# Second norm of a one-layer backbone taken in two token halves, with wider modulation rows

## The chip, the cores and the metric

The kernel runs on one core of a Trainium2 chip. Its engines work side by side: TensorE (PE, with its weight loads PEld), VectorE (DVE), ScalarE (ACT), GpSimd (POOL) and SyncE (SP); here POOL and SP mostly issue transfers. The metric is the device time of one launch in microseconds (us), the median of several.

## The reference

One layer (256 latent tokens, 256 context tokens, width 2048), float32, weights in float32:

```python
sh1_x, sc1_x, g1_x, sh2_x, sc2_x, g2_x = split(silu(c) @ w_mod + b_mod, 6)   # adaLN; the same from c_ctx
hx = rmsnorm(x) * norm1_g * (1 + sc1_x) + sh1_x          # hc from the context tokens
zx, zc = hx @ w_in + b_in, hc @ w_in + b_in
mix = concat(s5(zx, zc), conv(zx), mlstm(zx, zc))        # three groups of heads
x = x + g1_x * (mix @ w_out)
hx2 = rmsnorm(x) * norm2_g * (1 + sc2_x) + sh2_x         # the second norm
x = x + g2_x * (silu(hx2 @ w_g) * (hx2 @ w_u)) @ w_ffn_out   # width 5632
out = rmsnorm(x) * norm_f_g
```

## The kernel before, in words

Activations lie with features on the partitions and the 256 tokens along the free side, in 16 row tiles (`KT`). All big weights come as one stream of 128x128 tiles in the order in which they are used (`tile_order`), eight to a chunk of 512 KB. SP fetches chunk c into one of three `raw` buffers; ACT rounds it to float32r (`whi`, a 128x1024 cast, L511) and DVE subtracts to get the rest (`wlo`, L477), three buffers each. A product is three float32r matmuls: `whi*hhi`, `whi*hlo`, `wlo*hhi` (`mm3`, L609), each with its own weight load; `mm2` (L616) takes hi and lo of the activations in one matmul of 512 columns. So TensorE walks through the stream once: first the S5, conv, key, value (V), query (Q) and gate columns of `w_in`, then the GLU, `w_out` in two passes, and the feed-forward in eight blocks.

A product of the other kind, in plain float32 (`native=True`: norm sums, S5, attention), is recorded as two matmuls.

Beside the stream run jobs, written as generators and stepped by a pump (`Sched`): the S5 scan, the conv, the attention and the modulation (`mod_job`, L1037), which makes the gate, shift and scale vectors of `w_mod` that the layer's second half needs (quarters q = 0 to 3). For q = 0 it uses TensorE. For q = 1 to 3 it takes blocks of 512 columns: 16 steps on DVE that add weight row times scalar into an accumulator (`macc`, L488; the first step on ACT), then four transposes on TensorE (L1067) and four sums on ACT. POOL fetches its weights (`wm`, 512 KB each, three buffers).

`Arrange` (L152) then makes the final order of every engine's queue from a list schedule with costs written by hand; the order is fixed, and each engine works through its own in turn. A matmul on float32r costs `6 + 0.4427 * cols` ns there (L288), an ACT copy `190 + 0.84 * n`. `ranks` shifts an instruction's priority, `pins` ties it to the one before it.

After the first stage, `s5_moves` (L1091) turns `zT` into `U` by sixteen 32x512 copies, half on DVE (L492), half on ACT (L511). In V (L1341) each pass of four banks ends with four additions on DVE into `vx`, which free the banks; the first Q product takes the next bank of the tag `m`.

Around the second norm: the second pass over `w_out` makes 16 tiles `ct` of `xres`, 24 matmuls of 256 columns each; `SumSq` (L1508) squares each on ACT and sums over features on TensorE. After ct = 15 come `rsqrt` (L625: Ln and Exp on ACT, three DVE operations), `make_h2` for row tile 0 (L1557) and the feed-forward's first block, which runs over `kt` with eight weight tiles (24 matmuls) for each `kt`, into four banks.

Of the kernel before, what the change touches and what calls it, by code (L numbers as in the profile page):

```python
# [17 lines left out]
D = 2048  # L18
# [28 lines left out]
MOD_PE = {(0, b) for b in range(4)}  # L47
# [57 lines left out]
C_ID, C_MF, C_MR, C_K, C_SELG, NCST = 0, 128, 256, 384, 512, 640  # L105
# [46 lines left out]
class Arrange:  # L152
# [122 lines left out]
    def account(self, k, i, e, size):  # L275
# [8 lines left out]
        elif e == "PE":  # L284
# [4 lines left out]
            if any(x[1].startswith(("whi", "wlo")) for x in size):  # L289
                self.main.add(k)  # L290
# [162 lines left out]
def hybrid_layer_kernel(ctx: ExitStack, tc: tile.TileContext, xt, ctxt, wm1, wmr, wst, wg, bvrow, pvd, cstd, s5p, out):  # L453
# [21 lines left out]
    def tt(o, a, b, op):  # L475
        sc.dve += 62 + 1.05 * n_of(o)
        return V.tensor_tensor(out=o, in0=a, in1=b, op=op)  # L477

    def ts(o, a, s1, op0, s2=None, op1=None):
        if op1 is None:  # L480
            V.tensor_scalar(o, a, s1, None, op0=op0)
        else:
            V.tensor_scalar(o, a, s1, s2, op0=op0, op1=op1)
        sc.dve += 62 + 0.6 * n_of(o)

    def stt(o, a, s, b, op0, op1):
        sc.dve += 62 + 1.05 * n_of(o)
        return V.scalar_tensor_tensor(o, a, s, b, op0=op0, op1=op1)  # L488
# [13 lines left out]
    def act(o, a, f, bias=0.0, scale=1.0, pin=False):  # L502
        i = S.activation(o, a, f, bias=bias, scale=scale)  # L503
# [5 lines left out]
    def acopy(o, a):  # L509
        sc.act += 190 + 0.84 * n_of(o)  # L510
        return S.copy(o, a)  # L511

# [3 lines left out]
    def mm(o, l, r, start, stop, native=False, tp=None, sgc=False, pin=False):  # L516
# [7 lines left out]
        sc.pe += (max(n * 4, 512) if native else max(n, 256)) / 2.36 / (1 if tp is None else 4)  # L524
# [21 lines left out]
    cst = sb.tile([128, C_SELG], F32, name="cst")  # L546
# [7 lines left out]
    maskf = cst[:, C_MF:C_MF + 128]  # L554
    maskr = cst[:, C_MR:C_MR + 128]
# [18 lines left out]

    def split(c):
        his[c] = sb.tile([128, CH * 128], F32R, name="whi", tag="whi", bufs=3)
        ahead(U_SPLIT, acopy(his[c], raw[c]))
        los[c] = sb.tile([128, CH * 128], F32R, name="wlo", tag="wlo", bufs=3)
        ahead(U_SPLIT, tt(los[c], raw[c], his[c], OP.subtract))
        for d in (raw, his, los):  # L580
            d.pop(c - 4, None)
# [43 lines left out]
    def rsqrt(o, ps, n, scale, eps, epsv):  # L625
# [3 lines left out]
        act(y, y, AF.Exp, scale=-0.5)  # L629
        stt(t, y, -0.5 * scale, y, OP.mult, OP.mult)  # L630
# [126 lines left out]
    def s5_params():  # L757
# [7 lines left out]
        def expo(x, e, em1):  # L765
            n, r, p = t(), t(), t()
# [6 lines left out]
            ni = pre.tile([128, 32], I32, name="ni", tag="ni")  # L773
            V.tensor_copy(ni, n)
            V.tensor_copy(n, ni.bitcast(F32))
# [7 lines left out]
            used[0] -= 3  # L783
# [132 lines left out]
    for kt in range(KT):  # L916
# [8 lines left out]
        if kt == 13:  # L925
            phase1[0] = False
            keep(nc.sync.dma_start(cst[:, 128:], cstd[:, 128:C_SELG]))
# [108 lines left out]

    def mod_job():  # L1037
      for q in range(4):
        while mst["go"] < q:
            yield 500  # L1040
        for b in range(4):
            on_pe = (q, b) in MOD_PE
            acc = sb.tile([128, 512], F32, name="macc", tag="macc", bufs=1)
            if on_pe:
                psm = bbank()
            for kp in range(0, 8, 2):
                w = [wm.pop((q, b, kp + i)).rearrange("p (k n) -> p k n", k=2) for i in range(2)]
                for j in range(4):
                    kt = 2 * kp + j
                    wj = w[j // 2][:, j % 2, :]  # L1050
                    s = cs[:, kt, 0:1]
                    if on_pe:
                        mm(psm[32 * j:32 * j + 32, :], cs[:, kt, :], wj, kt < 4, kt >= 12, native=True, tp=(0, 32 * j),
                           pin=j > 0)
                    elif kt == 0:
                        act(acc, wj, AF.Copy, scale=s, pin=q == 3)
                    else:
                        stt(acc, wj, s, acc, OP.mult, OP.add)
                mod_dma()
                mod_dma()  # L1060
                yield 2 * (MOD_PACE if on_pe else MOD_PACE_D if q < 3 else MOD_PACE_F)
            dst = mods[:, q, 4 * b:4 * b + 4]
            if on_pe:
                acopy(acc, psm)
# [4 lines left out]
            if on_pe:  # L1069
                rsum(dst, ps.rearrange("p (f j r) -> p f j r", f=4, j=4)[:, :, :, 0])  # L1070
            else:
                for j in range(4):
                    S.activation(acc[:, 128 * j:128 * j + 128], ps[:, 128 * j:128 * j + 128], AF.Copy,
                                    accum_out=dst[:, j:j + 1])
                    sc.act += 390
# [265 lines left out]
    for cb in range(2):  # L1341
        pss = [mbank(), mbank(), mbank(), qbank()]
# [12 lines left out]
        for t in range(4):  # L1355
# [8 lines left out]
    hn = RH[:, 6144:8192].rearrange("p (j n) -> p j n", j=2)  # L1364

# [141 lines left out]
    stt(A2, mods[:, 2, :], 1.0, pvc("n2g", 0, 16), OP.add, OP.mult)  # L1507
    class SumSq:  # L1508


        def __init__(self):
            self.b = bank("qk", 2)
            self.sq = []
            self.n = 0
# [9 lines left out]
        def sums(self):  # L1524
            if self.n <= 12 and len(self.sq) == 4:
# [4 lines left out]
                if self.n == 12:  # L1530
                    e = tmp(256)
                    acopy(e, self.b[:, 0:256])
                    mm(self.b[:, 256:512], r32.to_broadcast([128, 128]), e, True, False, native=True)
            elif self.n > 12:
                mm(self.b[:, 256:512], ones, self.sq.pop(0), False, self.n == KT, native=True)
            return self.b[:, 256:512]

    s2 = SumSq()
    for ct in range(KT):
# [4 lines left out]
        if ct == 14:  # L1544
            lnexp()
# [3 lines left out]
    stp = s2.sums()  # L1549

# [3 lines left out]
    rsqrt(rs2, stp, 256, 1.0 / D, eps6, 1e-6)  # L1554
    h2 = sb.tile([128, KT, 2, NT], F32R, name="h2", tag="hc")

    def make_h2(kt):  # L1557
        xn, h = tmp(256), tmp(256)
        tt(xn, xres[:, kt, :], rs2, OP.mult)
        act(h2[:, kt, 0, :], xn, AF.Identity, bias=mods[:, 1, kt:kt + 1], scale=A2[:, kt:kt + 1])  # L1560
        ts(h, xn, A2[:, kt:kt + 1], OP.mult, mods[:, 1, kt:kt + 1], OP.add)
        tt(h2[:, kt, 1, :], h, h2[:, kt, 0, :], OP.subtract)
# [19 lines left out]
    def ffn_in(b):  # L1582
# [3 lines left out]
        if b == 0:  # L1586
            pss = [mbank(), mbank(), mbank(), qbank()]
            for kt in range(KT):
# [161 lines left out]
```

## Time and profile before

| | us |
|---|---|
| three runs, median | 1446.77 (1446.09 to 1446.86) |
| the profiled execution, its own time | 1447.56 |
| its span, first to last instruction | 1445.8 |
| TensorE busy | 1404.1 (97%) |
| DVE busy | 1049.0 (73%) |
| ACT busy | 738.3 (51%) |
| mean granted TensorE clock | 0.993 |

A row of the timeline gives start, duration, engine, line, operation and tiles; in brackets, how long the engine was idle before it and what it waited for. A duration of a matmul includes its way through the pipeline, so the time that one costs in a stream is read from start to start, or from a stretch of time divided by the matmuls in it.

### The profile page before, as it was taken

What the parts mean: (1) busy time and instruction counts of PE and PEld (TensorE: products, weight loads), DVE (VectorE), ACT (ScalarE), POOL (GpSimd) and SP (SyncE); (2) the same over time, 40 slices, a digit from 0 to 9 for tenths busy, and PEclk for the clock granted to TensorE, in tenths of its full rate; (3) what the DMA queues carried; (4) which work ended last, traced back from release to release, by engine and by line L of the source; (5) the groups of instructions that cost most, each with busy time, mean ns of one, the idle gap of its engine ahead of it and who ended that gap; (6) DMA issues with size and microseconds to landing.
All of it is one profiled execution on the core that took longest, in us unless ns stands there. A gap on an engine that the chain in (4) does not pass through costs nothing.

```text
span 1445.8 us, 25513 instructions
## 1 busy us (share of the span) xinstructions
PE 1404.1 (97%) x9920; PEld 1234.9 (85%) x9920; DVE 1049.0 (73%) x1944; ACT 738.3 (51%) x1302; POOL 107.7 (7%) x207
## 2 busy tenths in 40 slices
PE   5999999999999999998999999999999999999996
PEld 3888888987879999997998888888888888888885
DVE  8555699998878877988787778566555665556665
ACT  5334887666664445445555545534444334444353
POOL 1221111110001101111010000000000000000000
PEclk9999999999999999999999999999999999999998
DMA  9997564453427667788478787555555555555553
GB/s 370 382 350 292 184 218 145 166 181 127 149 77 293 214 234 269 246 302 290 161 276 275 255 286 261 187 186 184 189 188 189 189 190 188 187 184 186 190 176 115
DMA packets 87929, 315.50 MB, mean 218 GB/s; under 512 B 10096, under 2 KB 10736, under 8 KB 87808
## 3 DMA queue, kind: packets, MB, share of 16 engines
q1 hardware_dynamic: 60912, 216.80, 44.3%
q0 software_dynamic: 26896, 97.07, 18.8%
q8 instruction: 78, 1.28, 0.3%
q14 instruction: 43, 0.35, 0.1%
HBM read 311.73 MB, written 2.10 MB: 217 GB/s over the span
## 4 chain that ended last, share of the span: by engine, by line
PE 74%; issue 14%; DMA 4%; DVE 3%; POOL 2%; ACT 2%; SPq 0%; POOLq 0%; DVEq 0%; ACTq 0%
PE ps_m L520 48%; PE ps_qk L520 18%; PE ps_b L520 8%; DMA wm<-in_wmr_dram 2%; POOL wm L650 1%; DVE macc L488 1%; DMA wmu<-in_wm_dram 1%; DVE wlo L477 1%; DMA wmt<-in_wm_dram 1%; DMA cr<-in_ctxt_dram 1%; ACT whi L511 1%; DMA raw<-in_wst_dram 0%; ACT U L511 0%; POOL wmu L650 0%; PE ps_b L1160 0%
## 5 line engine op out<-in xcount | busy, mean ns | idle before, releaser
L477 DVE TENSOR_TENSOR wlo<-raw,whi 128x1024 fp32r<-128x1024 f32 x386 | 471.5, 1222 | 263.7 <-ACT whi L511 257.7
L511 ACT CAST whi<-raw 128x1024 fp32r<-128x1024 f32 x386 | 403.8, 1047 | 460.3 <-PE ps_m L520 231.7
L520 PE MATMUL ps_m<-h,whi 128*128 128x512 f32 (+1 forms) x800 | 252.1, 369 | 3.6 <-ACT h L503 3.5
L520 PE MATMUL ps_m<-ffa,whi 128*128 128x512 f32 x704 | 248.2, 395 | 0.0
L520 PE MATMUL ps_qk<-h,whi 128*128 128x512 f32 (+1 forms) x688 | 232.8, 383 | 0.0
L520 PE MATMUL ps_m<-h,wlo 128*128 128x256 f32 x704 | 199.6, 284 | 0.0
L520 PE MATMUL ps_m<-ffa,wlo 128*128 128x256 f32 x704 | 198.4, 282 | 0.0
L520 PE MATMUL ps_m<-hx,whi 128*128 128x256 f32 x960 | 186.3, 290 | 5.1 <-ACT hx L503 3.1
L520 PE MATMUL ps_qk<-h,wlo 128*128 128x256 f32 x656 | 185.5, 283 | 0.0
L520 PEld LDWEIGHTS ps_m<-h,whi 128*128 128x128 f32 x800 | 145.0, 190 | 30.4 <-ACT h L503 3.9
L520 PEld LDWEIGHTS ps_m<-hx,whi 128*128 128x128 f32 x960 | 148.2, 189 | 20.3 <-issue 15.3
L520 PEld LDWEIGHTS ps_m<-ffa,whi 128*128 128x128 f32 x704 | 132.3, 188 | 31.8 <-issue 1.2
L520 PEld LDWEIGHTS ps_qk<-h,whi 128*128 128x128 f32 x688 | 127.0, 188 | 27.1
L488 DVE SCALAR_TENSOR_TENSOR macc<-wm,cs,macc 128x512 f32<-128x512 f32 x180 | 134.3, 746 | 11.8 <-DMA wm<-in_wmr_dram 8.3
L520 PE MATMUL ps_m<-hx,wlo 128*128 128x256 f32 x480 | 136.5, 284 | 0.6 <-DVE wlo L477 0.6
L520 PEld LDWEIGHTS ps_m<-h,wlo 128*128 128x128 f32 x704 | 133.1, 189 | 0.0
L520 PEld LDWEIGHTS ps_m<-ffa,wlo 128*128 128x128 f32 x704 | 132.2, 188 | 0.1
L520 PEld LDWEIGHTS ps_qk<-h,wlo 128*128 128x128 f32 x656 | 123.3, 188 | 0.0
L650 POOL DMA_DIRECT2D wm<-in_wmr_dram x128 | 67.5, 528 | 585.1 <-DVE macc L488 436.4
L488 DVE SCALAR_TENSOR_TENSOR xres<-ps_m,mods,xres 128x256 f32<-128x256 f32 x160 | 76.9, 481 | 33.2 <-PE ps_m L520 31.2
L520 PEld LDWEIGHTS ps_m<-hx,wlo 128*128 128x128 f32 x480 | 90.6, 189 | 3.0 <-issue 2.1
L488 DVE SCALAR_TENSOR_TENSOR XB<-XB,pv 128x256 f32<-128x256 f32 x120 | 54.0, 477 | 0.4
(271 smaller groups left out, 2109.2 us busy)
## 6 DMA issues: line engine op xcount, KB each, us to landing
raw<-in_wst_dram SPq DMA_DIRECT2D x386, 512.0 KB, 3.6
wm<-in_wmr_dram POOLq DMA_DIRECT2D x128, 512.0 KB, 5.2
wm<-in_wm_dram POOLq DMA_DIRECT2D x24, 512.0 KB, 7.6
wmu<-in_wm_dram POOLq DMA_DIRECT2D x16, 512.0 KB, 7.6
wmt<-in_wm_dram POOLq DMA_DIRECT2D x8, 512.0 KB, 7.3
wms<-in_wm_dram POOLq DMA_DIRECT2D x7, 512.0 KB, 6.9
xr<-in_xt_dram SPq DMA_DIRECT2D x4, 512.0 KB, 5.5
cr<-in_ctxt_dram SPq DMA_DIRECT2D x4, 512.0 KB, 8.5
```

Source lines behind the costliest of these rows:

```text
L477: return V.tensor_tensor(out=o, in0=a, in1=b, op=op)
L488: return V.scalar_tensor_tensor(o, a, s, b, op0=op0, op1=op1)
L511: return S.copy(o, a)
L520: i = P.matmul(o, lhsT=l, rhs=r, start=start, stop=stop, skip_group_check=sgc, **kw)
L650: i = (q or nc.gpsimd).dma_start(wm[key], src)
```

## The change

Five things change.

- **Two token halves around the second norm.** The last two tiles of `w_out` (ct = 14, 15) are computed for tokens 0 to 127, then again from the same weights for tokens 128 to 255; norm, `rsqrt` and `h2` of row tiles 0 and 1 follow for each half, and the feed-forward's first block takes kt = 0 and 1 for one half, then for the other. From kt = 2 on it runs as before. Two chunks of weights are held longer and the next two are cast at fixed places (`split_hi`, `split_lo`, pinned). The instructions of the norm get a higher priority (`boost`), and the sums of the two halves lie in two banks.
- **Wider modulation rows.** For q = 1 to 3 the weights are packed in rows of 1024 columns; a step takes 128x1024 and a block has 1024 columns, so half as many steps and blocks, eight transposes for each; the job's pace gets a factor of 0.85.
- **Copies.** `s5_moves` puts 12 of its 16 copies on DVE and 4 on ACT.
- **Banks.** The second pass of V takes its first bank from the tag `qk` and frees it last.
- **Small ones.** The attention's masks are loaded after V into a part of `RH` (one 128 KB transfer on SP) instead of with the constants; a small tile in the S5 parameters is dropped.

```diff
@@ s5_moves
-                if (s + q) % 2:
+                if (s + q) % 4:
                     ahead(U_MOVE, vcopy(o, i))
                 else:
                     ahead(U_MOVE, acopy(o, i))
@@ modulation
+    def mod_wide(q, b, acc):
+        for kt in range(KT):
+            w = wm.pop((q, b + kt // 8, kt % 8))
+            s = cs[:, kt, 0:1]
+            if kt == 0:
+                act(acc, w, AF.Copy, scale=s, pin=q == 3)
+            else:
+                stt(acc, w, s, acc, OP.mult, OP.add)
+            if kt % 2:
+                mod_dma()
+                mod_dma()
+                yield 2 * (MOD_PACE_D if q < 3 else MOD_PACE_F) * MODW
+        dst = mods[:, q, 4 * b:4 * b + 8]
+        for i in range(2):
+            ps = bbank()
+            for j in range(4):
+                P.transpose(ps[:, 128 * j:128 * j + 128], acc[:, 512 * i + 128 * j:512 * i + 128 * j + 128], ident)
+            for j in range(4):
+                S.activation(acc[:, 512 * i + 128 * j:512 * i + 128 * j + 128], ps[:, 128 * j:128 * j + 128], AF.Copy,
+                             accum_out=dst[:, 4 * i + j:4 * i + j + 1])
+        tt(dst, dst, pvc("bm", 32 + 16 * q + 4 * b, 8), OP.add)
@@ V
-        pss = [mbank(), mbank(), mbank(), qbank()]
+        pss = [mbank(), mbank(), mbank(), qbank()] if cb == 0 else [qbank(), mbank(), mbank(), mbank()]
...
-        for t in range(4):
+        for t in (0, 1, 2, 3) if cb == 0 else (1, 2, 3, 0):
@@ masks
+    maskf, maskr = RH[:, 5888:6016], RH[:, 6016:6144]
+    nc.sync.dma_start(RH[:, 5888:6144], cstd[:, C_MF:C_MF + 256])
@@ second norm
-    for ct in range(KT):
+    for ct in range(KT - 2):
...
+    ws = [nxt() for _ in range(16)]
+    halves = []
+    for c in HALF:
+        for ct in range(KT - 2, KT):
+            ps = mbank() if c.start == 0 else bbank()
+            for i in range(8):
+                mm3(ps[:, 0:128], ws[8 * (ct - KT + 2) + i], (mixm[:, i, 0, c], mixm[:, i, 1, c]), i == 0, i == 7)
+            halves.append((c, ct, ps))
+            if len(halves) == 4 or len(halves) == 2:
+                boost[0] = BOOST
+                for c1, ct1, ps1 in halves[-2:]:
+                    stt(xres[:, ct1, c1], ps1[:, 0:128], mods[:, 0, ct1:ct1 + 1], xres[:, ct1, c1], OP.mult, OP.add)
+                sq = tmp(256)
+                act(sq.rearrange("p (k n) -> p k n", k=2), xres[:, KT - 2:KT, c], AF.Square)
+                for k in range(2):
+                    ahead(1, mm(s2.parts[c.start // 128][0], ones, sq[:, 128 * k:128 * k + 128], False, k == 1, native=True))
+                rsqrt(rs2[:, c], s2.parts[c.start // 128][0], 128, 1.0 / D, eps6, 1e-6,
+                      (lambda: split_hi(ca + 3, True)) if c.start == 0 else None)
+                for kt in range(2):
+                    make_h2(kt, c)
+                boost[0] = 0
+                if c.start == 0:
+                    split_lo(ca + 3, True)
+                    fetch_to(ca + 4)
+                    split_hi(ca + 4, True)
+                    split_lo(ca + 4, True)
@@ first feed-forward block
-            for kt in range(KT):
+            ws = [nxt() for _ in range(2 * 2 * FHEAD)]
+            for c in HALF:
+                for kt in range(2):
+                    hh = (h2[:, kt, 0, c], h2[:, kt, 1, c])
+                    for i in range(FHEAD):
+                        for g in range(2):
+                            mm3(pss[i][:, 256 * g + c.start:256 * g + c.stop], ws[2 * FHEAD * kt + 2 * i + g], hh,
+                                kt + g + c.start == 0, False, sgc=True)
+            for kt in range(2, KT):
                 make_h2(kt)
```

## Rows read from the trace of the kernel before

**Rows 1.** The page, busy us of each engine (share of the span) and instructions.

```profile
PE 1404.1 (97%) x9920; PEld 1234.9 (85%) x9920; DVE 1049.0 (73%) x1944; ACT 738.3 (51%) x1302; POOL 107.7 (7%) x207
```

**Rows 2.** Busy time in a stretch of the feed-forward's first block (x: instructions; then PEclk).

```profile
696.66:731.00 34.34, 34.34 (x291) 34.34 (x290) 22.50 (x36) 17.92 (x22) 0.00 (x0) 1.00 0.56 184
```

**Rows 3.** Timeline of TensorE around the second norm.

```profile
669.57 0.58 PE L520 MATMUL ps_m<-mixm,whi 128*128 128x256 f32 x2
...
679.05 0.70 PE L520 MATMUL ps_qk<-tmp,kc 128*128 128x256 f32 x2 [0.95 <-ACT tmp L503]
683.23 0.39 PE L520 MATMUL ps_m<-h,whi 128*128 128x256 f32 x1 [3.48 <-ACT h L503]
...
690.98 0.40 PE L520 MATMUL ps_m<-h,whi 128*128 128x256 f32 x2
```

**Rows 4.** Granted clock (the figure after the counts) in two stretches.

```profile
158.10:161.50 3.40, 3.40 (x16) 3.40 (x17) 2.43 (x3) 3.37 (x9) 0.00 (x0) 0.50 0.66 187
683.80:687.20 3.40, 3.40 (x16) 3.40 (x17) 3.40 (x11) 1.43 (x3) 0.00 (x0) 0.50 0.02 5
```

**Rows 5.** Timeline of TensorE at the start of conv.

```profile
156.78 0.50 PE L520 MATMUL ps_b<-hx,whi 128*128 128x256 f32 x2 [1.68 <-ACT whi L511]
158.04 0.53 PE L520 MATMUL ps_b<-hx,wlo 128*128 128x256 f32 x1 [0.75 <-DVE wlo L477]
```

**Rows 6.** Timeline of ACT in the same place.

```profile
147.78 7.89 ACT L511 COPY U<-zT 32x512 f32<-32x512 f32 x7
155.69 1.04 ACT L511 CAST whi<-raw 128x1024 fp32r<-128x1024 f32 x1
```

**Rows 7.** Copies into U, groups by shape (busy us, mean ns; idle before).

```profile
L492 DVE COPY U<-zT 32x512 f32<-32x512 f32 x8 | 4.9, 617 | 1.9 <-ACT zT L503 1.8
L511 ACT COPY U<-zT 32x512 f32<-32x512 f32 x8 | 8.9, 1119 | 0.1
```

**Rows 8.** Weight loads, groups by shape: float32r, then plain float32.

```profile
L520 PEld LDWEIGHTS ps_m<-mixm,whi 128*128 128x128 f32 x256 | 39.5, 189 | 1.4 <-issue 0.8 <-DVE macc L488 0.4
L520 PEld LDWEIGHTS ps_b<-tmp,Mb 128*128 128x128 f32 x128 | 16.0, 191 | 0.4
```

**Rows 9.** Timeline of weight loads: plain-float32 matmuls of 128 columns, then of 64.

```profile
168.22 0.97 PEld L520 LDWEIGHTS ps_b<-U,Wi 128*128 128x128 f32 x8
...
177.06 0.97 PEld L520 LDWEIGHTS ps_b<-tmp,Mb 128*128 128x128 f32 x8
```

**Rows 10.** Timeline of DVE and ACT in the second norm.

```profile
677.71 0.48 DVE L488 SCALAR_TENSOR_TENSOR xres<-ps_m,mods,xres 128x256 f32<-128x256 f32 x1 [0.60 <-PE ps_m L520]
679.79 0.47 ACT L503 ACTIVATE tmp<-ps_qk,kc 128x256 f32<-128x256 f32 x1 [0.79 <-PE ps_qk L520]
...
680.75 0.42 DVE L488 SCALAR_TENSOR_TENSOR tmp<-tmp 128x256 f32<-128x256 f32 x1 [0.81 <-ACT tmp L503]
682.58 0.60 ACT L503 ACTIVATE h<-tmp,mods,A 128x256 fp32r<-128x256 f32 x1 [1.86 <-DVE tmp L477]
```

**Rows 11.** Smaller shapes elsewhere, groups by shape.

```profile
L488 DVE SCALAR_TENSOR_TENSOR U<-U,pv,ps_b 128x64 f32<-128x64 f32 x16 | 4.4, 275 | 2.9 <-PE ps_b L520 2.7
L503 ACT ACTIVATE RH<-ps_b,acol 128x128 f32<-128x128 f32 x8 | 2.9, 368 | 7.0 <-DVE RH L483 7.0
L477 DVE TENSOR_TENSOR RH<-RH,qh 128x128 f32<-128x128 f32 x16 | 4.5, 284 | 1.9 <-ACT RH L503 1.8
```

**Rows 12.** Modulation steps, the group by shape.

```profile
L488 DVE SCALAR_TENSOR_TENSOR macc<-wm,cs,macc 128x512 f32<-128x512 f32 x180 | 134.3, 746 | 11.8 <-DMA wm<-in_wmr_dram 8.3 <-ACT macc L503 2.0
```

**Rows 13.** Waits of TensorE over the whole span (us in total, times, longest).

```profile
PE ps_b L1067 <- DVE macc L488: 3.1, 3, 1.4
...
PE ps_m L520 <- DVE vx L477: 2.0, 1, 2.0
...
PE ps_m L520 <- DVE wlo L477: 1.7, 3, 1.0
```

**Rows 14.** The same steps by tile, from 300 to 700 us (min/median/max ns).

```profile
L488 DVE SCALAR_TENSOR_TENSOR macc<-wm,cs,macc x120: 718/745/754, 349.2 to 674.1; 128x512 f32<-128x512 f32 x120
```

More of the change, by code (lines that the diff above doesn't have):

```diff
@@ L46 @@
 LEAD_R, LEAD_S = 2, 1
-MOD_PE = {(0, b) for b in range(4)}
+MOD_PE = {0}
+MODW = 0.85
+BOOST = 300
 def tile_order():
@@ L288, in account @@
             c = 6 + 0.4427 * cols if f32r else 109.0 if i.is_transpose else 2 * max(0.8438 * cols, 110.0)
-            if any(x[1].startswith(("whi", "wlo")) for x in size):
+            if i.name in self.ranks or any(x[1].startswith(("whi", "wlo")) for x in size):
                 self.main.add(k)
@@ L573, in raw_dma, with split_hi, split_lo @@
             keep(i)
-    def split(c):
[L576 to L581, printed above, removed]
+    def split_hi(c, pin=False):
+        his[c] = sb.tile([128, CH * 128], F32R, name="whi", tag="whi", bufs=3)
+        i = acopy(his[c], raw[c])
+        if pin:
+            keep(i)
+    def split_lo(c, pin=False):
+        los[c] = sb.tile([128, CH * 128], F32R, name="wlo", tag="wlo", bufs=3)
+        i = tt(los[c], raw[c], his[c], OP.subtract)
+        if pin:
+            keep(i)
+        for d in (raw, his, los):
+            d.pop(c - 5, None)
+    def split(c):
+        split_hi(c)
+        split_lo(c)
     def fetch_to(c):
@@ L623, in lnexp, with rsqrt @@
         keep(S.preload_act_table_set("natural_log_exp_and_others"))
-    def rsqrt(o, ps, n, scale, eps, epsv):
+    def rsqrt(o, ps, n, scale, eps, epsv, between=None):
         y, t = tmp(n), tmp(n)
@@ L629, in rsqrt @@
         act(y, y, AF.Exp, scale=-0.5)
+        if between:
+            between()
         stt(t, y, -0.5 * scale, y, OP.mult, OP.mult)
@@ L772, in expo @@
             ts(n, n, 8388608.0, OP.mult, 127.0 * 8388608.0, OP.add)
-            ni = pre.tile([128, 32], I32, name="ni", tag="ni")
-            V.tensor_copy(ni, n)
-            V.tensor_copy(n, ni.bitcast(F32))
+            V.tensor_copy(ni.bitcast(I32), n)
+            V.tensor_copy(n, ni)
             ts(p, r, 1.0 / 40320, OP.mult)
@@ L1040, in mod_job @@
             yield 500
[L1041 to L1045, printed above, removed]
+        for b in range(0, 4, 1 if q in MOD_PE else 2):
+            on_pe = q in MOD_PE
+            acc = sb.tile([128, 1024], F32, name="macc", tag="macc", bufs=1)
+            if not on_pe:
+                yield from mod_wide(q, b, acc)
+                continue
+            acc = acc[:, 0:512]
+            psm = bbank()
             for kp in range(0, 8, 2):
@@ L1068, in mod_job @@
                 sc.pe += 110
[L1069 to L1075, printed above, removed]
+            rsum(dst, ps.rearrange("p (f j r) -> p f j r", f=4, j=4)[:, :, :, 0])
             tt(dst, dst, pvc("bm", 32 + 16 * q + 4 * b, 4), OP.add)
@@ L1507, in hybrid_layer_kernel, with __init__ @@
     stt(A2, mods[:, 2, :], 1.0, pvc("n2g", 0, 16), OP.add, OP.mult)
+    HALF = [slice(0, 128), slice(128, 256)]
     class SumSq:
-        def __init__(self):
+        def __init__(self, halves=False):
             self.b = bank("qk", 2)
+            self.parts = [(self.b[:, 256:512], slice(0, 256))]
+            if halves:
+                self.parts = [(bank("qk", 2)[:, 0:128], HALF[0]), (self.b[:, 256:384], HALF[1])]
             self.sq = []
@@ L1548, in hybrid_layer_kernel @@
         s2.add(xres[:, ct, :])
-    stp = s2.sums()
+    lnexp()
+    s2.sums()
     prestack.close()
@@ L1659, in pack @@
     a["wmr"] = np.ascontiguousarray(mr.transpose(3, 4, 0, 2, 1, 5)).reshape(4, 4, 8, 128, 1024)
+    mw = wmod[:, 4096:].reshape(2, 8, 128, 4, 2, 1024).transpose(3, 4, 0, 1, 2, 5).reshape(4, 4, 8, 128, 1024)
+    for q in range(4):
+        if q not in MOD_PE:
+            a["wmr"][q] = mw[q]
     mats = {"in": f["w_in"][0][:, :OFF_G], "out": f["w_out"][0], "glu": f["s5_w_glu"][0], "ffi": f["w_ffn_in"][0],
```

74 lines of the change are left out of this document (39 added, 35 removed).

## The prediction

> **What bounds the kernel now.** I read the page first: TensorE is busy 97% of the span, DVE 73%, ACT 51% [rows 1]. So a microsecond is won only where TensorE stands still, runs at its lower clock, or has less to do. Next, what TensorE does when nothing disturbs it: in a quiet stretch of the feed-forward's first block it gets through 291 matmuls of 256 columns in 34.34 us, 0.118 us each [rows 2]. Against that pace I looked, in the timeline of TensorE, for the places where it falls behind.
>
> The largest is the second norm. Tile ct = 14 of the projection starts at 669.57, row tile kt = 2 of the feed-forward at 690.98: 21.41 us for 96 weight matmuls that would take 96 x 0.118 = 11.3 at the quiet pace. In it TensorE waits 0.95 us for a square and 3.48 us for the first `h2` [rows 3], and right after that it gets half its clock: granted 0.50 from 683.8 to 687.2 [rows 4], that is 1.2 instead of 2.4 GHz, after a stretch in which it did little but two norm sums. 3.4 us at half speed lose 1.7.
>
> The second is at the start of conv: again 0.50 of the clock for 3.4 us, another 1.7 [rows 4], and ahead of it waits of 1.68 us for a `whi` cast and 0.75 for the next `wlo` [rows 5]. What ACT did instead of the cast is plain: seven copies into `U` in a row, 7.89 us, and only then the cast at 155.69, though TensorE ran dry at about 156.78 - 1.68 = 155.1 [rows 5, 6].
>
> **The change, part by part.**
>
> *Copies into U.* A copy takes 617 ns on DVE and 1119 on ACT [rows 7]; the code's own cost for ACT is 190 + 0.84 x 512 = 620, so the written order lets the cast come later than it plans. Four copies instead of eight free ACT 4 x 1.12 = 4.5 us earlier: the cast, 1.04 us long, starts at about 151.2 and is done well before 155.1. Both waits go. They are 2.4 us as rows, and 2.7 in the stream, because each begins only when the last matmul's 0.28 us of pipeline are over, not its 0.118. With no gap ahead of it the clock should stay (1.7). That is -4.4. DVE gets 4 x 0.62 = 2.5 us more, just where it is waiting for the same cast; were that cover gone, the `wlo` behind would be 2.5 late and the gain 2. Bounds 0 and -4.4; I take -4.4, because the cast has 4.5 us to come forward and needs 2.7.
>
> *Matmuls of 128 columns.* The halves turn 96 weight matmuls of 256 columns into 192 of 128, with 192 weight loads. No float32r matmul of 128 columns is in the trace, so I bound it. Below: half of 0.118, 0.059 us, if columns alone count. The nearest rows are the loads. A float32r load of 128x128 is as long as a plain-float32 one, 189 and 191 ns [rows 8]. Eight plain-float32 loads take 0.97 us, so (0.97 - 0.19) / 7 = 0.111 from one to the next, and the same 0.97 whether 128 or only 64 columns go with each [rows 9]: there the load sets the pace, not the columns. With 256 columns a load of 0.111 hides behind them; with 128 it can't. I take 0.111 us each, almost the price of the whole matmul. Above: two such records, as a plain-float32 matmul has, 0.222. A half of two tiles is then 48 x 0.111 = 5.3 us, and the four halves 21.3.
>
> The Trainium skill says otherwise (TensorE: Matmul & The Clock Gate, Back-to-back issue gap): pairs of load and matmul at N = 128 run at about 81 ns. By it the four halves would be an estimated 15.6 us, 5.7 less than I sum. The same page's section on LDWEIGHTS gives a load of 128 columns as 128 / 1.2 = 107 ns, which is nearly what the loads here show. So the page speaks for both prices, and the rows for the second; the first is a rival below.
>
> *The chain of the norm in halves.* In the old trace 5.52 us pass from the last update of `xres` at 677.71 to the first `h2` matmul at 683.23 [rows 3, 10]. At 128 columns its parts shrink: the update from 0.48 to about 0.34 and each of four DVE operations from 0.42 to 0.28 [rows 10, 11], Ln (0.47), Exp and the `h2` cast (0.60) by about 0.1 each as the columns halve [rows 10]: 1.0 in all, so about 4.5. With 0.3 of hand-over ahead of it that is less than the 5.3 us that TensorE has to do meanwhile. So the halves do cover the chain; and with no gap the clock should stay up.
>
> So this stretch: 21.3 + sums 1.3 (three norm sums, each two records of 0.22) = 22.6, plus what the fixed order gets wrong. That order was planned with 6 + 0.4427 x 128 = 63 ns for a matmul that takes 111, so the sums sit at the wrong place in TensorE's queue; the fourth bank of the feed-forward's first block, from the tag that both halves' sums hold, may come free only when the second `rsqrt` has read it; `split_hi` stands on ACT behind Exp until the second half has left chunk ct = 14, with the `h2` casts queued behind it, and TensorE behind those. Each costs between 0 and 2; I take 0.8 in all. Before: 21.41, less 1.0 of waiting for modulation and 0.6 of its transposes, which are counted below: 19.8. Net 2.8 + 0.8 = **+3.6: this part makes the kernel slower**, since the matmuls that cover the stall are work that wasn't there before.
>
> *Wider modulation rows.* A step of 512 costs 746 ns [rows 12]; the same operation costs 0.48 at 256 [rows 10], so 512 more columns are 0.53 and a wide step 1.28. 90 of them are 115 us instead of 134: 19 us of DVE, most of it hidden behind TensorE. What TensorE sees are the transposes that wait for a block's last step: 3.1 us in three places [rows 13]. Half as many blocks: -1.55; bounds 0 (a longer last step) and -3.1. DVE's slack also shows where `wlo` is late, 1.7 us in all [rows 13]: -0.5, bounds 0 and -1.7. The steps for q = 1 and 2 run from 349.2 to 674.1, right up to the norm [rows 14]; 325 x 0.85 is 276, so they should end near 625.
>
> *Banks of V.* TensorE waits 2.0 us for `vx` at the change to Q [rows 13]. The new order drains another bank first, whose last matmul is three of 0.23 us later, and the DVE step that may stand ahead of it is longer. Bounds +0.7 and -2; I take -1.0.
>
> *At nothing:* the masks' 128 KB go on SP, and the `raw` fetches queue behind them while they wait for the end of V; three buffers of 2.8 us each cover that (used up, one chunk is late by up to 2 us). The first constant transfer is smaller by as much. The dropped tile leaves the two copies that used it.
>
> Sum, against the profiled execution: 1447.56 - 4.4 - 1.55 - 0.5 - 1.0 + 3.6 = 1443.7. It lies 0.8 above the median of the runs; against that, about **1443.0 us**.
>
> **The rivals.**
>
> *The halves run by columns.* Then TensorE's half is 2.8 us (0.059) to 3.8 (0.08), shorter than the chain, and the chain shows twice: the stretch is about 14.5 to 17.8 us instead of 23.4, and the time 1434 to 1437.4. For it: in the 256-column stream only 0.118 - 256 / 2400 = 0.011 us stand over the columns, so loads overlap well. Against it: the 64-column rows. The skill's 81 ns is this case.
>
> *Plain-float32 pace (the other side).* If float32r with so few columns takes as many passes as plain float32, a matmul is 0.222: four halves 42.6 us, 21.3 more: 1464. It decides from about 0.15 us a matmul: there the stretch loses 7.5 more, and the sum is over 1450. For it: at 128 columns the trace knows only that path. Against it: a float32r matmul is one record, and its 256 columns take 0.118.
>
> *The copies change nothing.* ACT's freed time is filled with other work that the new order puts ahead of the cast, the wait and the half clock stay: 1443.0 + 4.4 = 1447.4, no change. For it: the remaining four copies are still planned at half their time. Against it: 4.5 us is much for a wait of 2.7.
>
> **How the numbers follow.** Forecast 0.53, halves by columns 0.20, plain-float32 pace 0.09, copies without effect 0.18. The forecast's own range is 1439.5 to 1446.5, from the bounds of modulation, banks and order. 1434.5 to 1448.5 holds it, the copies rival and most of the columns rival, and leaves out under 2 in 10. A measurement of this kernel can tell some 0.2%, 2.9 us, from no change: faster is below 1443.9, slower above 1449.7. The forecast puts six tenths of itself below 1443.9 (0.31), the columns rival all (0.20), the copies rival little (0.02): faster 0.53; slower 0.11 (0.09, and 0.02 of order waits on top of one another); same 0.36.
>
> **What would show it.** Start to start of the 128-column float32r matmuls: 0.111 right, 0.06, 0.08 or 0.22 a rival. No wait of TensorE above 0.5 us near 155 and 680, and no granted 0.50 in either place. From the first half of ct = 14 to kt = 2: 23 to 24 us. Waits of L1067 halved, steps of 1.28 us that end near 625. I am wrong if the halves cost other than 0.10 to 0.13, or if a new wait of over 2 us appears (fourth bank, pinned cast, `vx`).

## The result and the profile after

The changed kernel takes 1461.56 us (median of four runs, 1459.15 to 1462.47); the kernel before took 1446.43 beside it. The ratio is 1.0098, with a 95% interval of 1.0086 to 1.0110: the change makes the kernel about 15 us slower. The forecast was 1443.0, the range 1434.5 to 1448.5. The profiled execution has a span of 1460.6. Below, "before" and "after" are the traces of the kernel before and of the changed kernel.

The first line of the page, to be held against [rows 1]: TensorE is busy 22 us longer, though the span grew by 15. So it isn't standing still more; it works more or slower.

```profile
PE 1425.8 (98%) x10026; PEld 1256.9 (86%) x10026; DVE 1042.0 (71%) x1863; ACT 733.5 (50%) x1296; POOL 108.0 (7%) x207
```

Where does it happen? Tile ct = 14 starts at 669.75, 0.2 later than before; row tile kt = 2 starts at 703.84, 12.9 later [rows 3]. The stretch between them has grown from 21.41 to 34.09 us, nearly all of what the span grew by. Three windows of after: the projection halves, the feed-forward halves, and the wide matmuls behind them (the granted clock stands after the counts).

```profile
669.75:681.30 11.55, 11.55 (x107) 11.55 (x105) 3.68 (x9) 4.94 (x8) 0.00 (x0) 1.00 0.25 77
682.60:703.80 21.20, 21.14 (x99) 21.14 (x100) 9.50 (x24) 5.89 (x11) 0.00 (x0) 0.50 0.22 73
706.50:740.00 33.50, 33.50 (x284) 33.50 (x284) 24.19 (x44) 17.22 (x22) 0.00 (x0) 1.00 0.56 175
```

The projection halves and the feed-forward halves have nearly the same number of matmuls of the same shape. The first run at 2.4 GHz and take 11.6 us, the second at 1.2 GHz and take 21.2. Before, the half clock here lasted 3.4 us [rows 4]; now it lasts over 21. It isn't an accident of the profiled execution: the mean granted clock of the four executions of the changed kernel lies between 0.984 and 0.987, that of the kernel before in the executions taken beside the experiments between 0.988 and 0.994. The timeline of TensorE shows both prices and what lies between them:

```profile
670.12 0.38 PE L529 MATMUL ps_m<-mixm,whi 128*128 128x128 f32 x2
670.34 0.28 PE L529 MATMUL ps_m<-mixm,wlo 128*128 128x128 f32 x1
...
681.40 0.27 PE L529 MATMUL ps_m<-h,whi 128*128 128x128 f32 x1
682.66 0.47 PE L529 MATMUL ps_m<-h,whi 128*128 128x128 f32 x1 [0.99 <-DVE h L479]
...
683.15 0.63 PE L529 MATMUL ps_m<-h,whi 128*128 128x128 f32 x2
683.58 0.41 PE L529 MATMUL ps_m<-h,wlo 128*128 128x128 f32 x1
...
703.84 0.73 PE L529 MATMUL ps_m<-h,whi 128*128 128x256 f32 x2
```

Two matmuls take 0.22 us from start to start at 670, 0.43 at 683. Between them stands one wait of 0.99 us. DVE's timeline tells why the low part of `h2` was late:

```profile
680.15 0.29 DVE L479 TENSOR_TENSOR tmp<-xres,rs 128x128 f32<-128x128 f32 x1
681.60 0.35 DVE L490 SCALAR_TENSOR_TENSOR xres<-ps_b,mods,xres 128x128 f32<-128x128 f32 x1 [1.15 <-PE ps_b L529]
681.87 0.34 DVE L485 TENSOR_SCALAR tmp<-tmp,A,mods 128x128 f32<-128x128 f32 x1
682.12 0.28 DVE L479 TENSOR_TENSOR tmp<-xres,rs 128x128 f32<-128x128 f32 x1
682.32 0.28 DVE L479 TENSOR_TENSOR h<-tmp,h 128x128 fp32r<-128x128 f32 x1
```

In DVE's fixed queue the update of `xres` for the second half stands ahead of the first half's `h2`. DVE waits 1.15 us for the last projection matmul, and TensorE, done with it, waits for DVE.

Elsewhere, the start of conv became in part what was forecast: the two waits for the weights are gone and the clock is 1.00 where [rows 4] had 0.50. But a wait of 0.76 us for `Wi`, a tile of the S5 job that ACT copies, has come in their place. V's first matmul comes 3.1 us earlier (313.66 against 316.71), but a group of S5 matmuls that stood ahead of it now stands behind it; at V's third matmul, with the same work done, the lead is 1.7 us (315.55 against 317.26). As after began conv 0.9 us later, the stretch is 2.6 us shorter. At the change from V to Q there is a half clock that the trace of before doesn't have; the last section shows that it can't be put down to the change. A row and two windows of after, at conv and at Q:

```profile
159.37 0.89 PE L529 MATMUL ps_b<-Mb,WR 128*32 128x128 f32 x32 [0.76 <-ACT Wi L513]
```

```profile
150.00:165.00 15.00, 14.24 (x145) 12.88 (x144) 10.94 (x17) 11.48 (x20) 1.49 (x3) 1.00 0.75 268
433.40:436.70 3.30, 3.30 (x18) 3.30 (x17) 3.30 (x5) 0.00 (x0) 0.00 (x0) 0.50 1.02 366
```

The wait ahead of the half clock at Q has grown from 2.0 [rows 13] to 2.8 us. A modulation step costs what was worked out, 1279 ns, and the wait of the transposes is gone (0.0 after the bar, in place of 3.1 [rows 13]). Groups of after, by tile and by shape:

```profile
L490 DVE SCALAR_TENSOR_TENSOR macc<-wm,cs,macc x90: 1252/1279/1286, 334.7 to 856.2; 128x1024 f32<-128x1024 f32 x90
```

```profile
L1073 PE MATMUL ps_b<-cst,macc 128*128 128x128 f32 x48 | 6.2, 272 | 0.0
```

### The profile page after: what moved, and what is told of

The parts are those of the page before. It is cut to its first block, busy times and chain, and to the rows that moved or that the text cites. A ratio compares the mean times of both kernels' runs of the same rounds, so it can differ in the third digit from the quotient of the medians.

```text
span 1460.6 us, 25617 instructions
## 1 busy us (share of the span) xinstructions
PE 1425.8 (98%) x10026; PEld 1256.9 (86%) x10026; DVE 1042.0 (71%) x1863; ACT 733.5 (50%) x1296; POOL 108.0 (7%) x207
## 4 chain that ended last, share of the span: by engine, by line
PE 85%; DVE 6%; DMA 3%; issue 3%; ACT 2%; POOL 1%; SPq 0%; DVEq 0%; POOLq 0%; ACTq 0%
PE ps_m L529 55%; PE ps_qk L529 20%; PE ps_b L529 9%; DMA raw<-in_wst_dram 1%; DVE wlo L479 1%; DVE XB L490 1%; DVE tmp L479 1%; DMA wm<-in_wm_dram 1%; ACT whi L513 0%; DVE Vr L479 0%; DMA xr<-in_xt_dram 0%; DVE tmp L490 0%; DMA bc<-in_s5p_dram 0%; ACT tmp L505 0%; DVE xres L479 0%
## 5 line engine op out<-in xcount | busy, mean ns | idle before, releaser
L529 PE MATMUL ps_m<-h,whi 128*128 128x512 f32 (+2 forms) x824 | 262.2, 373 | 1.0 <-DVE h L479 1.0
L529 PE MATMUL ps_qk<-h,whi 128*128 128x512 f32 (+2 forms) x696 | 236.3, 385 | 0.0
L529 PE MATMUL ps_m<-h,wlo 128*128 128x256 f32 (+1 forms) x716 | 206.0, 288 | 0.0
L529 PE MATMUL ps_qk<-h,wlo 128*128 128x256 f32 (+1 forms) x660 | 187.7, 284 | 0.0
L529 PEld LDWEIGHTS ps_m<-h,whi 128*128 128x128 f32 x824 | 154.0, 198 | 27.4 <-DVE h L479 1.1
L529 PEld LDWEIGHTS ps_qk<-h,whi 128*128 128x128 f32 x696 | 130.1, 191 | 27.1
L529 PEld LDWEIGHTS ps_m<-h,wlo 128*128 128x128 f32 x716 | 138.7, 194 | 0.0
L490 DVE SCALAR_TENSOR_TENSOR macc<-wm,cs,macc 128x1024 f32<-128x1024 f32 x90 | 115.1, 1279 | 10.9 <-DMA wm<-in_wmr_dram 9.0
L490 DVE SCALAR_TENSOR_TENSOR xres<-ps_m,mods,xres 128x256 f32<-128x256 f32 (+1 forms) x160 | 76.9, 480 | 44.1 <-PE ps_m L529 42.0
```

Source lines behind the costliest of these rows:

```text
L490: return mark(V.scalar_tensor_tensor(o, a, s, b, op0=op0, op1=op1))
L529: i = P.matmul(o, lhsT=l, rhs=r, start=start, stop=stop, skip_group_check=sgc, **kw)
```

## The experiments

Three theories of the lost time were set against each other. A: a stream of 128-column matmuls brings the clock down by itself. B: a wait brings it down, and the narrow stream behind the wait keeps it down. C: narrow matmuls with the feed-forward's operands cost 0.21 at any clock.

**Without the halves** (the second norm and first feed-forward block of before in the changed kernel).

```diff
-    s2 = SumSq(True)
-    for ct in range(KT - 2):
+    s2 = SumSq()
+    for ct in range(KT):
...
-            ws = [nxt() for _ in range(2 * 2 * FHEAD)]
-            for c in HALF:
...
-            for kt in range(2, KT):
+            for kt in range(KT):
```

> The changed kernel with the second norm and the first feed-forward block of the kernel before; copies, wide modulation rows, banks and masks stay as changed. If the halves are what lost the time (both theories of how), the 12.9 us that the trace of after lost between ct = 14 and kt = 2 come back, and the kernel ends between 1445 and 1449 us; the old wait of about 3.5 us for the first h2 and a half clock of 3.4 us near 680 are there again. Rival: the loss belongs to the modulation or the priorities, which crowd the stretch in any form: then it stays above 1455.

Measured: 1445.97 us against 1447.54, ratio 0.9987 (0.9977 to 0.9996). The loss belongs to the halves. What is left of the change is worth 1.9 us (0.6 to 3.3), not the 7.45 that I had summed for it. The wait of 3.48 us for the first `h2` is back as expected; the half clock behind it lasts not 3.4 but 6.8 us in this trace (from 678.5 on).

**Copies alone**, in the kernel before.

```diff
-                if (s + q) % 2:
+                if (s + q) % 4:
```

> The kernel before with 12 of the 16 copies into U on DVE and 4 on ACT, nothing else. By my sum it gains 4.4 us: about 1442, no wait of TensorE above 0.5 us near 155 and no granted 0.50 near 158. Rival: the start of V comes 3 to 4 us earlier, but other work queues at the change from V to Q and takes it back: 1445 to 1447.

Measured: 1443.91 against 1447.54, ratio 0.9977 (0.9968 to 0.9986), a gain of 3.3 us (2.0 to 4.6); the 4.4 of the sum lies inside. V's first matmul starts 4.1 us earlier in the trace, but ahead of an S5 group that stood ahead of it before; at V's third matmul, with the same work done, the lead is 2.8 us (314.50 against 317.26). The half clock near 158 is gone as expected, but not every wait above 0.5 us: one of 0.74 us for `Wi` at 158.79 is new. Behind V the trace has other losses: a `wlo` 1.77 us late and a half clock behind it, and after the norm's wait a half clock of 6.6 us at least, where [rows 4] had 3.4. Two windows and a row of this run:

```profile
585.10:588.40 3.30, 3.30 (x17) 3.30 (x17) 2.69 (x5) 0.00 (x0) 0.59 (x2) 0.50 0.95 315
...
677.30:683.90 6.60, 4.67 (x20) 4.41 (x21) 5.90 (x17) 2.40 (x4) 0.00 (x0) 0.50 0.21 71
```

```profile
583.73 0.39 PE L520 MATMUL ps_m<-mixc,wlo 128*128 128x256 f32 x1 [1.77 <-DVE wlo L477]
```

**A narrow stream without a wait.** In the kernel before, one pair of feed-forward tiles in pieces of 128 columns.

```diff
+    def mm2n(o, w, h, first, last):
+        whi, wlo = w
+        for s in range(2):
+            for t in range(2):
+                c = slice(128 * t, 128 * t + 128)
+                mm(o[:, 256 * s + 128 * t:256 * s + 128 * t + 128], whi, h[:, s, c], first and s + t == 0, False, sgc=True)
+        for t in range(2):
+            c = slice(128 * t, 128 * t + 128)
+            mm(o[:, c], wlo, h[:, 0, c], False, last, sgc=True)
...
-                    mm2(ps, nxt(), h2[:, kt], kt == 0, kt == KT - 1)
+                    if b == 1 and i == 4:
+                        mm2n(ps, nxt(), h2[:, kt], kt == 0, kt == KT - 1)
+                    else:
+                        mm2(ps, nxt(), h2[:, kt], kt == 0, kt == KT - 1)
```

> The kernel before; in the second feed-forward block one of the pairs of gate and up tiles is computed in matmuls of 128 columns: 192 of them in a row in place of 64 larger ones, the same products, no wait ahead of them. At 0.112 us each the stretch takes 21.4 us instead of some 10.7. Theory A, such a stream lowers the clock by itself: the granted clock falls to 0.50 within the stretch, a matmul costs 0.21 there, and the kernel ends over 15 us later than the kernel before. Theory B, the fall needs a wait ahead of it: clock 1.00 all through, 0.112 each, about 10.7 us later. Theory C, a matmul with the feed-forward's operands costs 0.21 at any clock: 1.00 granted and 0.21 each.

The window over all 192 matmuls (and six others) in this run:

```profile
855.28:877.00 21.72, 21.72 (x198) 21.72 (x196) 10.81 (x15) 7.00 (x17) 1.59 (x3) 1.00 0.56 177
```

Clock 1.00 from end to end, 21.7 us for 192 and the six others, and a span 10.9 us longer than before: 1456.7, in one execution. That is B's number. A and C fall: neither the stream nor its operands make it slow.

**A wait, then wide; a wait, then narrow.** Same place, same products. Three DVE operations add zero times the last result to the first activation tile, so that TensorE must stand still. One execution each.

```diff
+    def late(ps, hk):
+        t = hk
+        for _ in range(3):
+            o = sb.tile([128, 512], F32R, name="tmp", tag="tmp", bufs=4)
+            o = o.rearrange("p (k n) -> p k n", k=2)
+            ahead(1, stt(o, ps.rearrange("p (k n) -> p k n", k=2), 0.0, t, OP.mult, OP.add))
+            t = o
+        return t
...
+                    hk = h2[:, kt]
+                    if b == 1 and i == 4 and kt == 0 and ps is pg:
+                        hk = late(pv0, hk)
+                    if NARROW and b == 1 and i == 4:
+                        mm2n(ps, nxt(), hk, kt == 0, kt == KT - 1)
+                    else:
+                        mm2(ps, nxt(), hk, kt == 0, kt == KT - 1)
+            pv0 = pu
```

`NARROW` is False in the first run and True in the second; `mm2n` is that of the run above.

> The kernel before; in the second feed-forward block, ahead of the same pair of tiles as in the run with a narrow stream, three DVE operations add zero times the last result to the first activation tile, so that TensorE must stand still for some 3 us; wide matmuls (512 and 256 columns) follow. Same products. Theory B: half clock for one or two stretches of 3.4 us after the wait, then full again: 4.5 to 6.5 us later than the kernel before. If a wait alone has no such effect: 3 us later and clock 1.00.

> The same wait of some 3 us, then the 192 matmuls of 128 columns in a row. Theory B: the clock falls after the wait as in the run with wide matmuls, but stays at 0.50 until the narrow stream ends: 192 x 0.213 = 40.9 us, 20 us more than the narrow stream without a wait, and a granted 0.50 of some 40 us. Rival: the clock comes back after the same 3.4 to 6.8 us as with wide matmuls, so that the long half clock of the changed kernel has another cause.

Wide matmuls behind the wait, timeline and two windows:

```profile
864.26 0.80 PE L521 MATMUL ps_m<-tmp,whi 128*128 128x512 f32 x1 [3.20 <-DVE tmp L489]
```

```profile
864.26:867.40 3.14, 3.13 (x9) 2.67 (x10) 2.86 (x4) 0.00 (x0) 0.95 (x2) 0.50 0.57 171
867.60:875.00 7.40, 7.40 (x45) 6.49 (x44) 5.15 (x7) 3.40 (x5) 0.98 (x2) 1.00 0.76 219
```

Narrow ones behind the same wait:

```profile
861.25 1.12 PE L521 MATMUL ps_m<-tmp,whi 128*128 128x128 f32 x4 [3.14 <-DVE tmp L489]
```

```profile
861.25:901.00 39.75, 39.74 (x187) 39.75 (x187) 11.86 (x15) 3.88 (x6) 2.53 (x5) 0.50 0.35 107
903.10:910.00 6.90, 6.90 (x41) 6.03 (x40) 5.48 (x10) 2.67 (x4) 0.00 (x0) 1.00 0.43 110
```

The waits are equal, 3.20 and 3.14 us, and in both runs two shorter ones, of some 0.6 to 0.8 us, stand just ahead. Behind the one the full clock is back by 867.60, 3.3 us after the work resumes; behind the other it stays at 0.50 through the whole narrow stream, 39.75 us, and comes back about 2 us after the wide matmuls do. Single times: 1457.29 and 1482.57, against 1458.51 for the narrow stream without a wait. With that run and the kernel before, all four combinations are there. The narrow stream alone costs 10.9 us of span, the wait alone 9.7, both together 35.0, 14 us more than the sum. The run with wide matmuls also had a difference that I hadn't asked for: other half clocks and a longer wait for transposes ahead of the place, worth some 2.9 of its 9.7 us (the same four transposes start at 821.15 in before and at 824.09 here). The rest, 6.8 us, is a little above the 4.5 to 6.5 expected; in the run with narrow ones that place is reached as in before (821.07).

**Whole feed-forward rows** in the changed kernel: kt = 0 and 1 at 256 columns, projection halves kept.

```diff
-            ws = [nxt() for _ in range(2 * 2 * FHEAD)]
-            for c in HALF:
...
-            for kt in range(2, KT):
-                make_h2(kt)
+            for kt in range(KT):
+                if kt > 1:
+                    make_h2(kt)
```

> The changed kernel, with the projection's last two tiles in token halves but kt = 0 and 1 of the feed-forward's first block over whole tokens, 256 columns a matmul: 48 matmuls at 0.118 = 5.7 us in place of 96. They have to wait for the second half's h2, about 4 us. Theory A (128-column stream lowers the clock): 96 such matmuls stand alone, then the wait; a half clock of 3.4 us or a little more, about 1449. Theory B (the wait lowers it, the 128 columns keep it there): half clock of about 3.4 us after the wait, since 256 columns follow; also 1446 to 1450. Rival C (price of the h2 halves at any clock): the whole 0.1 a matmul comes back, the same time; but no half clock. What tells most is how long the granted 0.50 lasts after a wait when wide matmuls follow: 3.4 us, against 23.9 with the halves.

Measured: 1452.15 against 1447.54, ratio 1.0036 (1.0024 to 1.0048). The waits of this form are longer, 1.73 and 2.77 us, and yet the half clock lasts half as long. Window and row of this run:

```profile
680.30:690.40 10.10, 6.67 (x29) 6.33 (x30) 8.80 (x24) 5.03 (x11) 0.00 (x0) 0.50 0.32 105
```

```profile
684.95 0.91 PE L529 MATMUL ps_m<-h,whi 128*128 128x256 f32 x2 [2.77 <-ACT h L505]
```

My expectation of 3.4 us was too short, since the clock was already low during the waits; the time lies 2 us above the 1446 to 1450 that I gave for B, and above A's 1449 too, so the time alone doesn't tell the two apart.

**One cost of the planner corrected**, the changed kernel otherwise whole.

```diff
-            c = 6 + 0.4427 * cols if f32r else 109.0 if i.is_transpose else 2 * max(0.8438 * cols, 110.0)
+            c = max(6 + 0.4427 * cols, 112.0) if f32r else 109.0 if i.is_transpose else 2 * max(0.8438 * cols, 110.0)
```

> The changed kernel, whole, with one number corrected: the planner counts a float32r matmul at no less than 112 ns, so that in the queue of DVE the second half's update of xres no longer stands ahead of the first half's h2. The wait of 0.99 us near 682 should go. Theory B (a wait is needed to bring the clock down): no granted 0.50 between 682 and 706, the 96 narrow matmuls of the feed-forward cost 0.112 instead of 0.213, 9.7 us, and with the wait about 10.8 us come back: near 1450.5. Theory A (192 narrow matmuls around a norm bring it down in any case): half clock again, less than 2 us gained, near 1460.

Measured: 1448.12 against 1447.44, ratio 1.0002 (0.9991 to 1.0013). Some 13 of the 15 us come back, 2.4 more than the 1450.5 expected. DVE's queue in this run has the last update of `xres` behind the first half's `h2`, with a `wlo` between them:

```profile
678.88 0.56 DVE L479 TENSOR_TENSOR h<-tmp,h 128x128 fp32r<-128x128 f32 x2
679.35 1.22 DVE L479 TENSOR_TENSOR wlo<-raw,whi 128x1024 fp32r<-128x1024 f32 x1
680.48 0.35 DVE L490 SCALAR_TENSOR_TENSOR xres<-ps_b,mods,xres 128x128 f32<-128x128 f32 x1
```

And the two windows, projection halves and feed-forward halves, both at full clock:

```profile
668.20:679.70 11.50, 11.50 (x106) 11.50 (x104) 5.15 (x15) 5.36 (x9) 0.00 (x0) 1.00 0.23 76
679.80:690.90 11.10, 11.10 (x101) 11.08 (x101) 9.73 (x25) 6.49 (x11) 0.00 (x0) 1.00 0.36 97
```

From ct = 14 to kt = 2 it takes 22.91 us (668.14 to 691.05), where the forecast had 23.4 and after has 34.09. The number moves more than one instruction of the planned order, and ct = 14 starts 1.6 us earlier here than in after for a reason that I didn't follow. But no TensorE wait is left in the stretch, and the mean granted clock of all ten executions is 0.993 to 0.996, against 0.984 to 0.987 for the changed kernel. Together with the four combinations above this shows the wait of 0.99 us, by way of the clock, as the cause of nearly all that was lost.

**Old bank order** (no halves, V's banks and drain as before).

```diff
-        pss = [mbank(), mbank(), mbank(), qbank()] if cb == 0 else [qbank(), mbank(), mbank(), mbank()]
+        pss = [mbank(), mbank(), mbank(), qbank()]
...
-        for t in (0, 1, 2, 3) if cb == 0 else (1, 2, 3, 0):
+        for t in range(4):
...
```

> The changed kernel with the second norm and first feed-forward block of the kernel before, and also with the banks and the order of the drain in V of before; left of the change are copies, wide modulation rows and masks. Against the run without halves it tells what the bank order is worth: if the order causes the longer wait at the change from V to Q (2.8 us against 2.0) and the half clock behind it (1.7), it is 2.5 us faster, about 1443.5, and beats the kernel before by some 3 us. If the order ahead of it on DVE (a wlo and a wide step) causes it, no change: 1446. Against the run with copies alone it tells what the wide rows are worth: 2 us by my prediction, so 1442; nothing or a loss, if V's longer work eats it.

Measured: 1444.88 against 1447.44, ratio 0.9981 (0.9971 to 0.9992). That lies between the two expected times, 1443.5 and 1446, and its interval holds both; against the run without halves (0.9987) the intervals overlap. The trace shows the wait at Q back at 1.99 us from 2.8: DVE now does the first three `vx` additions ahead of the wide step (428.86 and 430.66), where the new order has the step first. So in the traces the new order costs some 0.8 us of waiting. The half clock stays all the same:

```profile
431.00:434.30 3.30, 3.30 (x17) 3.30 (x17) 3.30 (x4) 0.43 (x2) 0.53 (x1) 0.50 0.95 334
```

Against copies alone (0.9977) it is no faster, so of the 2 us expected of the wide rows nothing shows.

**Wide rows and moved masks alone** in the kernel before.

```diff
-MOD_PE = {(0, b) for b in range(4)}
+MOD_PE = {0}
+MODW = 0.85
...
+    def mod_wide(q, b, acc):
```

> The kernel before with the wide modulation rows and the moved masks alone: old copies, old banks, old norm. By my prediction the fewer blocks and the freer DVE are worth 2.05 us: 1445.4 and two waits of L1067 at most. Rival, from the run with copies and wide rows, which was no faster than copies alone: the wide rows bring nothing that TensorE sees, 1447 to 1448, because longer steps of DVE stand ahead of what TensorE waits for elsewhere.

Measured: 1447.96 against 1447.35, ratio 0.9997 (0.9988 to 1.0006). That is the rival's time. The transposes' wait is gone (0.1 for the group, 3.1 before) and the wait at Q is 1.3 instead of 2.0; but waits for `wlo` are 2.9 us in four places instead of 1.7 in three, and two waits for DVE's `RH` in the attention, 2.0 us together, are new. By these rows some 0.5 us would be left, which the time can't tell from nothing.

**Copies, and the norm's waits filled** with matmuls that nobody reads, in the kernel before.

```diff
+NWARM = 27
...
-                if (s + q) % 2:
+                if (s + q) % 4:
...
+    warm = bbank()
+    for j in range(7):
+        mm(warm[:, 0:256], mixm[:, 0, 0, 0:128], mixm[:, 1, 0, :], True, True, pin=True)
     stp = s2.sums()
+    for j in range(NWARM):
+        mm(warm[:, 0:256], mixm[:, 0, 0, 0:128], mixm[:, 1, 0, :], True, True, pin=True)
```

> The kernel before with the copies into U as changed, and with 34 matmuls of 256 columns whose result nobody reads in the two waits of the second norm: 7 before the last norm sum (wait of 0.95 us), 27 after it (3.48 us). At 0.118 us each they take 4.0 us that TensorE spends waiting anyway. Theory B (the wait brings the clock down, the work behind it only decides how long it stays down): no granted 0.50 near 680, where the run with copies alone had 6.8 us of it, so 3.4 us come back: near 1440.5, and faster than both kernels. Rival: such matmuls do not keep the clock up, or they delay the first h2 matmul: 1443.5 to 1446.

Measured: 1443.01 against 1447.35, ratio 0.9971 (0.9960 to 0.9983), the lowest of all runs and below both kernels. The timeline and two windows show the wait filled and the clock at 1.00, during it and behind it:

```profile
674.78 1.18 PE L521 MATMUL ps_b<-mixm 128*128 128x256 f32 x7
676.08 0.70 PE L521 MATMUL ps_qk<-tmp,kc 128*128 128x256 f32 x2
676.43 3.58 PE L521 MATMUL ps_b<-mixm 128*128 128x256 f32 x27
680.27 0.38 PE L521 MATMUL ps_m<-h,whi 128*128 128x256 f32 x1 [0.26 <-ACT h L504]
```

```profile
674.78:680.20 5.42, 5.11 (x38) 4.62 (x36) 3.88 (x8) 2.73 (x5) 0.00 (x0) 1.00 0.84 280
681.00:687.40 6.40, 6.40 (x55) 6.40 (x56) 5.99 (x17) 4.12 (x7) 0.00 (x0) 1.00 0.11 12
```

From the first h2 matmul to kt = 2 it takes 6.24 us (680.27 to 686.51) instead of 8.11 with copies alone (679.23 to 687.34): 1.9 us, not 3.4, since part of the old half clock had lain over the wait itself. The clock did what B says, the time didn't: it lies 2.5 us above B's 1440.5. The run can't be told apart from copies alone, since their intervals overlap and both profiled executions have a span of 1442.1: the norm starts 1.0 us later here, for reasons ahead of it. What filling is worth to the whole kernel isn't shown.

## Why the prediction was wrong

**The step that failed** is "So the halves do cover the chain; and with no gap the clock should stay up." There was a gap. In the changed kernel TensorE waited 0.99 us for the first half's `h2`, and from there the granted clock was 0.50 for over 21 us, a term that the sum doesn't have. I had seen that the order was planned with 63 ns for a matmul that takes 111, and looked for what it would misplace among the sums, the fourth bank and the cast; it was the second half's `xres` update on DVE. I gave the order 0.8 us in all. The wait itself was 0.99, near that, and under the 2 us that I had named as the sign of being wrong. What I left out is what a wait does ahead of a narrow stream: the granted clock stays at 0.50 until the narrow matmuls are over. I had taken 3.4 us of half clock from [rows 4] as the price of any wait, though those rows were all followed by wide or mixed work. That is the difference between 22.91 and 34.09 us in the stretch, and 1.2 more until the clock is back, within kt = 2.

The Trainium skill (TensorE: Matmul & The Clock Gate, What's actually happening) says that the time at the low clock is a fixed amount of time, not a number of matmuls. The runs here don't bear that out: behind equal waits the granted clock stayed at 0.50 for 3.1 us with wide matmuls and for 39.75 us with narrow ones.

**Price of a narrow matmul**: right. 0.112 from start to start at full clock, in the projection, in the stream without a wait and in the corrected order. At the half clock the columns count even less: from 704.59 to 705.23 of after three matmuls of 256 columns take 0.64 us, the same as three of 128 from 683.15 to 683.79. The columns rival (0.06 to 0.08) is out. The plain-float32 rival had the right size for the time, 1464, by a mechanism that isn't there: the 0.213 of the feed-forward halves is the half clock. That it came so near the measured 1461.56 is luck.

**Sum of the stretch**: 23.4 forecast, 22.91 with the wait removed. Halves that work as meant still don't pay: 1448.12 against 1445.97 without them, 2.2 us (by the two intervals some 0.1 to 4.3), where I had forecast 2.8 and 0.8 for the order.

**Copies into U**: right in mechanism and size, 3.3 us (2.0 to 4.6) alone for 4.4. Both waits and the half clock went (all five traces with the old copies have a half clock near 158, none of the seven with the new ones does); the new wait of 0.74 us for `Wi` is a term that the sum doesn't have.

**Modulation**: the step's cost is right, and the transposes' waits went altogether (3.1, not 1.55). Of the forecast 2.05 us the time shows 0.4, with an interval that holds zero. The half of the term that failed is `wlo`: with wide steps it came later, not earlier, and so did `RH`, which the sum doesn't have. In the changed kernel the last steps before the norm start at 632.9, for the 625 that I gave.

**Banks of V**: wrong sign. The wait grew from 2.0 to 2.8 us, the end of my bound (+0.7), not -1.0: the step that I named, a wide one of 1.28 us, and a `wlo` do stand ahead of `vx` on DVE, where before a step of 0.74 and a `wlo` stood:

```profile
429.59 1.23 DVE L479 TENSOR_TENSOR wlo<-raw,whi 128x1024 fp32r<-128x1024 f32 x1 [0.77 <-PE ps_m L529]
430.74 1.28 DVE L490 SCALAR_TENSOR_TENSOR macc<-wm,cs,macc 128x1024 f32<-128x1024 f32 x1
431.93 1.88 DVE L479 TENSOR_TENSOR vx<-ps_m,bvb 128x512 f32<-128x512 f32 x3
```

So without the step that failed the change would still have been worth nothing (1.0002) rather than the forecast gain: 7.45 less 3.6 became 1.9 less 2.2.

## What to carry to other kernels

Before you split matmuls into narrow ones to cover a stall, ask what happens if the cover fails by a microsecond: here a wait of 0.99 us cost some 12, because the narrow stream behind it ran at the low clock to its end. Where an order is laid down by a planner, give it the measured price of every new shape first; one number took back 13 us. A stall that can't be removed can be filled with wide matmuls that nobody reads: in the one trace of it the clock stayed up, and the work behind took 1.9 us less, without any of the halves' extra work. A gain in the kernel's time wasn't shown.

## What the hardware showed unexpectedly

With a wait of 3.14 us ahead, narrow float32r matmuls (128 columns) ran at a granted 0.50 for 39.75 us, to the end of their stream. Behind waits followed by wide ones 0.50 was granted for about 3 to 10 us. Without a wait the same narrow stream ran 21.7 us at 1.00.

What makes a given wait bring the clock down stays open. Waits of 0.99 (after, 682), 1.77 (copies, 583) and 1.99 us (old banks, 430) did. Ahead of the first of these the stream was narrow too; no run tells whether so short a wait would have sufficed behind wide matmuls. In the kernel before, a wait of 0.96 us ahead of 587.71 and one of 1.98 ahead of 431.43 did not, as its windows behind them show:

```profile
587.70:592.00 4.30, 4.29 (x37) 4.29 (x38) 4.30 (x7) 0.68 (x1) 0.53 (x1) 1.00 0.58 172
431.40:435.00 3.60, 3.57 (x30) 3.60 (x31) 3.60 (x6) 0.72 (x2) 0.00 (x0) 1.00 0.86 308
```

So the length of the wait alone doesn't decide. Nor does the program: the run with a wait and a narrow stream differs from the kernel before only in the feed-forward's second block, and TensorE's wait and DVE's operations at the change from V to Q are the same, but here the half clock follows:

```profile
431.21 0.47 PE L521 MATMUL ps_m<-hx,whi 128*128 128x256 f32 x2 [1.98 <-DVE vx L478]
```

```profile
432.00:435.30 3.30, 3.30 (x18) 3.30 (x17) 3.30 (x5) 0.00 (x0) 0.00 (x0) 0.50 0.70 269
```

Half clocks of this length, worth 1.7 us each, therefore can come and go between traces, and the one at Q in after can't be put down to the change; the run with whole feed-forward rows, with the order of after at this place and a wait of 2.76 us, doesn't have it. The mean granted clock of the kernel before ranges from 0.988 to 0.994 in the 61 executions beside the experiments, its time from 1444.37 to 1451.17 us. The long half clock of the changed kernel doesn't come and go like that: the mean clocks of its four executions lie below all of these, those of the corrected order's ten at 0.993 or above.
